# One decoder layer on one core: sample bias rows stored once a head and token, the sweep's weight loads issued by GpSimd, and a third eviction tile

## The chip, the cores and the metric

The kernel runs on one core of a Trainium2 chip. The metric is device time in microseconds of one execution. Three executions of the kernel before took 3164.48, 3169.32 and 3171.83 us; the median, 3169.32 us, is what the change is measured against.

## The reference

One inference step of one decoder layer, for a prompt of 2048 rows and for 8 x 4 = 32 sample rows that share all weights. In outline:

```
h = RMSNorm(x) @ w_in          # 1024 -> 9472 columns: q, k, v, za, u (GLU), zb, qc, zc, 3 merge gates
A: dilated window attention, 12 heads x 64, patterns (128,1), (512,4), (2048,16), combined by their denominators
B: GLU -> causal depthwise conv, width 31 -> LayerNorm -> swish
C: cross-attention, 4 heads x 128, into 256 memory rows
mix = sum over A, B, C of sigmoid(gate) * ((branch * silu(z)) @ w_proj)
y = x + RMSNorm(mix @ w_out)
```

In the sample path of A the 32 rows look into a cache of 1024 past keys. To each score comes a bias that depends on the head, on the token t = 0..3 (through the distance from the key), and on the pattern. All data is fp32. The outputs also hold the new key and value rows, the conv state and the memory keys and values.

## The kernel before, in words

**Products.** Every fp32 product is made of three matmuls on float32r parts: `gemm` (L156 to L164) multiplies the high part of the weights with the high and the low part of the activations, and the low part of the weights with the high part. `load_w` (L141 to L154) loads 128 columns of a weight (128 partitions x 8 blocks of 512 bytes, 512 KB) as `wraw` and splits it into `whi` and `wlo`; the split of the input projection's weights is done by GpSimd, in two instructions (L55, L56). Activations lie in SBUF by thirds of the rows (`THIRDS`: 768, 768, 544).

**Phases.** `phase_a1` (to about 860 us) normalises x, builds bias tables (`bias_rows`), and makes q, k, v, qc and the GLU with its convolution. Then three strands run side by side until about 2560 us: (1) `memory`, which holds `memory_kv`, the LayerNorm of the conv branch in chunks of 256 rows (`conv_norm`), the prompt's cross-attention and the sample's; then `sample_bias` and `sample_attention`; (2) `attention`, six pairs of heads; (3) `sweep`, which makes the remaining 40 blocks of 128 columns (za, zb, zc and the gates gt) for each third, and is the filler of the other two. `phase_c` then makes the output projections; it is not touched by the change.

**The order of the work.** The program is emitted strand after strand, and a planner with a simulated time line then orders each engine's instructions by priority; the sweep is emitted last and fills what the others leave. On the chip each engine, and each engine's queue of DMA issues, runs its list strictly in that order. A DMA that waits for a semaphore therefore holds back everything behind it on the engine that issues it.

**The sweep** (L1064 to L1080). Per third, X is reloaded by GpSimd (16 DMAs at L1072); per block, `load_w` is called with `q=nc.scalar`, so that ScalarE issues the load of `wraw` (L146). There are two `wraw`, two `whi` and two `wlo`: the load of block n+2 waits until GpSimd has read `wraw` of block n (the end of its L56). The chunks of a block (`SCHUNKS`: seven of 256 rows, one of 288) go through `chunk` (L223 to L242): 24 matmuls into one of two PSUM tiles `gg`, then ScalarE makes tanh into an eviction tile `st` (L237 for the gates, L239 for the z paths), for the z paths VectorE multiplies it with the PSUM tile (L240), and ScalarE issues the store of `st` (L242). In the sweep there are two `st` tiles of 128 x 384, of which a chunk uses 256 or 288 columns. An `st` is free when its store has landed, and a `gg` when L237 or L240 has read it.

**The sample bias.** `bias_rows` (L344) makes a table `exs` of 12 heads x 3 patterns x 752 values and stores it to DRAM in one DMA (L368). `sample_bias` (L678 to L700) builds for each pattern a tile `sb` of 112 partitions x 672: partitions 0 to 47 and 64 to 111 are (head, token), and a token's row is the table's row shifted by 3 - t. It does so with 56 loads that SyncE issues (L695, L696, L698), each for 12 partitions of one token; three copies on VectorE (L699) then spread four values per row from `sn`. The tiles are first read in `sample_attention` (L802, L803).

**The combine of a head pair** (`att_pair`, L407) uses two small tiles of 32 x 128: `mn` (L417) for the minimum over patterns and `wsum` (L425) for the sum of weights. `mn` is last read before `wsum` is first written, by the same engine.

Of the kernel before, what the change touches and what calls it, by code (L numbers as in the profile page):

```python
# [7 lines left out]
F32 = mybir.dt.float32  # L8
# [4 lines left out]
PSUM = bass.MemoryType.PSUM  # L13
# [6 lines left out]
HA, DA, EA = 12, 64, 768  # L20
# [3 lines left out]
NT_S = 752  # L24
# [4 lines left out]

GROUPS = [(0, 3), (3, 6), (6, 9), (9, 12), (12, 14), (14, 17)]  # L30
CHUNKS = [(0, 384), (384, 384), (768, 384), (1152, 384), (1536, 256), (1792, 288)]
SCHUNKS = [(256 * i, 256) for i in range(7)] + [(1792, 288)]
THIRDS = [(0, 768), (768, 768), (1536, 544)]

CQ, CK, CV, CZA, CUB, CZB, CQC, CZC, CGT = 0, 768, 1536, 2304, 3072, 4608, 5376, 5888, 6400
# [2 lines left out]
class K:  # L38
# [184 lines left out]
    def chunk(self, kind, j, s, n, w, stg, psg, tag, pst=None, q=None):  # L223

        nc = self.nc
        q = q or nc.sync
        p = psg.tile([128, 512], F32, name=tag)
        self.gemm(p[:, :n], w, [self.x_at(k, s, n) for k in range(8)])
        st = stg.tile([128, 384], F32, name="st")
        dst = dict(q=self.d_q, k=self.d_k, qc=self.d_qc, za=self.d_za, zb=self.d_zb, zc=self.d_zc, gt=self.d_g).get(kind)  # L230
        if kind in ("q", "k", "v", "qc"):
            sc = dict(q=-0.125, k=1.0, qc=float(np.float32(DC ** -0.5)), v=1.0)[kind]
            nc.scalar.activation(st[:, :n], p[:, :n], AF.Copy, scale=sc)  # L233
            if kind in "kv":
                self.rows_out(kind, j, s, n, st, stg, pst)
        elif kind == "gt":
            nc.scalar.activation(st[:, :n], p[:, :n], AF.Tanh, scale=0.5)  # L237
        else:
            nc.scalar.activation(st[:, :n], p[:, :n], AF.Tanh, scale=0.5)  # L239
            nc.vector.scalar_tensor_tensor(st[:, :n], st[:, :n], 1.0, p[:, :n], op0=ALU.add, op1=ALU.mult)  # L240
        if dst is not None:
            q.dma_start(dst[j][:, s:s + n], st[:, :n])  # L242
# [101 lines left out]
    def bias_rows(self, cpool, pool, psum):  # L344
        nc, I = self.nc, self.I
        rb = self.rb = cpool.tile([33, HA], F32, name="rb")
        nc.vector.memset(rb, 1.0e30)
        raw = pool.tile([32, HA], F32, name="rbr")
        nc.sync.dma_start(raw, I["rel_bias"])
        nc.vector.tensor_scalar(rb[0:32], raw, -1.0, None, op0=ALU.mult)  # L350
        oh = pool.tile([33, 3, 384], F32, name="oh")
        nc.sync.dma_start(oh, I["c_onehot"])
        ext = pool.tile([HA, 3, 384], F32, name="ext")
        for p in range(3):
            t = psum.tile([128, 512], F32, name="tr")
            nc.tensor.matmul(t[:HA, :384], rb, oh[:, p, :], start=True, stop=True)
            nc.vector.tensor_copy(ext[:, p, :], t[:HA, :384])
        nc.sync.dma_start(self.d_ext, ext)
        ohs = pool.tile([33, 3, NT_S], F32, name="ohs")
        nc.sync.dma_start(ohs, I["c_onehot_s"])  # L360
        exs = pool.tile([HA, 3, NT_S], F32, name="exs")
        for p in range(3):
            for c in range(0, NT_S, NT_S // 2):
                cs = slice(c, c + NT_S // 2)
                t = psum.tile([128, 512], F32, name="tr")
                nc.tensor.matmul(t[:HA, :NT_S // 2], rb, ohs[:, p, cs], start=True, stop=True)
                nc.vector.tensor_copy(exs[:, p, cs], t[:HA, :NT_S // 2])
        nc.sync.dma_start(self.d_exs, exs)  # L368
        pf = pool.tile([128, 3, 128], F32, name="permf")
        nc.sync.dma_start(pf, I["c_perm"])  # L370
        self.perm = cpool.tile([128, 3, 128], R32, name="perm")
        nc.vector.tensor_copy(self.perm, pf)
# [34 lines left out]
    def att_pair(self, hp):  # L407
        nc, ap, ps, ao = self.nc, self.ap, self.aps, self.ao
# [13 lines left out]
        nc.scalar.activation(e, e, AF.Exp, scale=-1.0)  # L422
        el = st[:, 3:6, :]
        nc.vector.tensor_mul(el, e, el)
        w = ao.tile([32, 128], F32, name="wsum")  # L425
        nc.vector.tensor_add(w, el[:, 0, :], el[:, 1, :])
        nc.vector.tensor_add(w, w, el[:, 2, :])
        nc.vector.reciprocal(w, w)
# [249 lines left out]
    def sample_bias(self, keep):  # L678

        nc = self.nc  # L680
        NK, R = 672, 112
        self.sbias = []
        for p in range(3):
            bt = keep.tile([R, NK], F32, name=f"sb{p}")
            nc.vector.memset(bt, 1.0e30 if p < 2 else 0.0)
            nw = keep.tile([R, 4], F32, name=f"sn{p}")
            nc.vector.memset(nw, 0.0)
            base = self.d_exs[:, p, :]
            for r in (0, 64):
                for t in range(4):  # L690
                    rows = slice(r + t, r + 48, 4)

                    def src(o, n):
                        return bass.AP(tensor=base.tensor, offset=base.offset + o, ap=[[base.ap[0][0], HA], [1, n]])
                    nc.sync.dma_start(bt[rows, 0:512], src(3 - t, 512))  # L695
                    nc.sync.dma_start(nw[rows, :], src(515 + 3 - t, 4))  # L696
                    if p == 2:
                        nc.sync.dma_start(bt[rows, 512:640], src(522 + 32 * (3 - t), 128))  # L698
            nc.vector.tensor_copy(bt[:, 640:NK].rearrange("p (b t) -> p b t", t=4), nw[:, None, :].to_broadcast([R, 8, 4]))  # L699
            self.sbias.append(bt)  # L700


    def sample_attention(self):
# [360 lines left out]
    def sweep(self, blocks, xp, wp, stg, ps):  # L1064
        nc = self.nc
        for th, (a, n) in enumerate(THIRDS):
            if th:
                X = ([], [])
                for k in range(8):
                    for c in range(2):  # L1070
                        t = xp.tile([128, 768], R32, name=f"x0{'hl'[c]}{k}")
                        nc.gpsimd.dma_start(t[:, :n], self.d_x[th][c][k])  # L1072
                        X[c].append(t)
                self.X[th] = X
            for kind, j in blocks:
                w = self.early.pop((kind, j), None) if th == 0 else None
                w = w or self.load_w(wp, self.win(self.BASE[kind] + 128 * j), 8, q=nc.scalar, bufs=2, rp=stg)
                for s, m in SCHUNKS:
                    if a <= s < a + n:
                        self.chunk(kind, j, s, m, w, stg, ps, "gg", q=nc.scalar)  # L1080
                        yield
# [108 lines left out]
    def build(self):  # L1190
        tc, nc = self.tc, self.nc
        with tc.tile_pool(name="dr", bufs=1, space=DRAM) as dp, tc.tile_pool(name="cst", bufs=1) as cp:
            self.scratch(dp)
            self.cpool = cp
            with tc.tile_pool(name="x0", bufs=1) as x0, tc.tile_pool(name="w1", bufs=2) as wp:
                self.X = [tuple([x0.tile([128, 768], R32, name=f"x0{c}{k}") for k in range(8)] for c in "hl"), None, None]
                self.phase_a1(wp)
                with tc.tile_pool(name="gst", bufs=2, reuse_waits="tile") as gp, tc.tile_pool(name="pgg", bufs=2, space=PSUM, reuse_waits="tile") as pgg:
                    blocks = [(k, j) for k, n in (("za", 6), ("zb", 6), ("zc", 4), ("gt", 24)) for j in range(n)]
                    self.filler, self.credit = self.sweep(blocks, x0, wp, gp, pgg), 0  # L1200
                    with tc.tile_pool(name="sbk", side="right", bufs=1, reuse_waits="tile") as sk:
# [7 lines left out]
    def scratch(self, dp):  # L1209
# [7 lines left out]
        self.d_c = t("d_c", [6, 128, T])  # L1217
        self.d_actb = t("d_actb", [6, 128, T])
        self.d_ext = t("d_ext", [HA, 3, 384])
        self.d_exs = t("d_exs", [HA, 3, NT_S])  # L1220
        self.d_st = [t(f"d_st{h}", [6, S]) for h in range(HA)]
        self.d_cf = [t(f"d_cf{j}", [3, 2 * S]) for j in range(6)]
        self.d_act = [None if 6 <= j < 12 else t(f"d_act{j}", [128, T]) for j in range(16)]
# [73 lines left out]
```

## Time and profile before

| | |
|---|---|
| median of three executions | 3169.32 us (3164.48 to 3171.83) |
| profiled execution | 3156.1 us; span 3154.0 us |
| TensorE busy | 2992.8 us, 95% of the span |
| VectorE, GpSimd, ScalarE busy | 65%, 43%, 36% |
| mean granted TensorE clock | 0.983 |

The profile is one execution. Times in it count from the start of its span. Busy shares leave out instructions that only issue a DMA or wait for a semaphore; a row whose engine is called ACTq or SPq is such an instruction in the queue of that engine. `[1.5 <-DVE st L240]` behind an instruction of the time line means that its engine sat idle for 1.5 us before it, until VectorE finished the instruction of line 240 that writes `st`. Such a releaser is inferred; where several were waited for, it is the last one.

### The profile page before, as it was taken

To read this page: it belongs to the slowest core of one execution; us is meant where nothing else is said; L and a number is where in the kernel's file an instruction comes from. 1 tells how busy PE (TensorE), PEld (TensorE's weight loads), DVE (VectorE), ACT (ScalarE), POOL (GpSimd) and SP (SyncE) were. 2 spreads that over 40 slices of the span, in tenths; PEclk is the share of its full clock that TensorE was granted. 3 is DMA by queue.
4 is the path that set the end of the run, shared out by engine and by line. 5 is a ranking of instruction groups with operands and counts; after the bars stand their busy time and mean duration, and the time that the engine had idled before them with its cause. 6 is when DMAs were issued, how large, how long until landed. Compare 5 with 4: busy or idle time off the path is not lost. (4 is left out here: it accounts for less than half of the span.)

```text
span 3154.0 us, 55551 instructions
## 1 busy us (share of the span) xinstructions
PE 2992.8 (95%) x20705; PEld 2837.2 (90%) x20705; DVE 2037.6 (65%) x3854; ACT 1123.6 (36%) x2835; POOL 1368.9 (43%) x1048
## 2 busy tenths in 40 slices
PE   7999999999977999999999999999999989999998
PEld 6899999999977899998999999999898967787897
DVE  5297797797677825565546667565757557555663
ACT  5110010010132423244447575665565532222221
POOL 0121322232455537444366666667776443233240
PEclk9999999999998999999999999999999999999999
DMA  6332222221255444468454556575655486657561
GB/s 224 111 100 83 80 60 61 63 63 64 90 162 166 127 140 144 147 213 251 144 142 118 151 139 159 123 196 144 166 140 149 117 283 210 226 172 220 158 206 53
DMA packets 532219, 454.67 MB, mean 144 GB/s; under 512 B 118191, under 2 KB 458581, under 8 KB 531137
## 3 DMA queue, kind: packets, MB, share of 16 engines
q1 hardware_dynamic: 357502, 335.36, 36.3%
q10 hardware_dynamic: 169840, 105.02, 11.6%
q0 software_dynamic: 4608, 10.75, 1.1%
q8 instruction: 164, 2.69, 0.4%
q14 instruction: 105, 0.86, 0.1%
HBM read 332.96 MB, written 118.04 MB: 143 GB/s over the span
## 5 line engine op out<-in xcount | busy, mean ns | idle before, releaser
L162 PE MATMUL gg<-x0h,whi 128*128 128x256 f32 (+1 forms) x2560 | 747.9, 292 | 33.9 <-DVE st L240 26.9
L164 PE MATMUL gg<-x0h,wlo 128*128 128x256 f32 (+1 forms) x2560 | 741.1, 290 | 5.7 <-POOL wlo L56 5.7
L163 PE MATMUL gg<-x0l,whi 128*128 128x256 f32 (+1 forms) x2560 | 742.3, 290 | 0.0
L55 POOL TENSOR_SCALAR whi<-wraw 128x1024 fp32r<-128x1024 f32 x162 | 221.4, 1368 | 918.0 <-PE g L163 534.7
L162 PEld LDWEIGHTS gg<-x0h,whi 128*128 128x128 f32 x2560 | 493.7, 193 | 42.2 <-DVE st L240 23.5
L164 PEld LDWEIGHTS gg<-x0h,wlo 128*128 128x128 f32 x2560 | 493.6, 193 | 8.3 <-POOL wlo L56 6.1
L163 PEld LDWEIGHTS gg<-x0l,whi 128*128 128x128 f32 x2560 | 493.9, 193 | 1.9 <-issue 0.3
L316 DVE SCALAR_TENSOR_TENSOR acc<-G,cw,acc 128x1536 f32<-128x1536 f32 (+15 forms) x354 | 461.8, 1336 | 0.0
L56 POOL TENSOR_TENSOR wlo<-wraw,whi 128x1024 fp32r<-128x1024 f32 x162 | 451.8, 2790 | 9.9 <-PE gg L164 0.5
L151 POOL TENSOR_TENSOR clo<-craw,chi 128x768 fp32r<-128x768 f32 (+1 forms) x96 | 172.6, 1799 | 352.9 <-ACT chi L150 338.1
L616 ACT ACTIVATE P<-T,stm 128x128 f32<-128x128 f32 (+1 forms) x576 | 260.7, 455 | 116.7 <-DVE stm L614 78.1
L233 ACT ACTIVATE st<-g 128x384 f32<-128x384 f32 (+1 forms) x132 | 60.3, 461 | 564.8 <-PE g L164 564.8
L614 DVE CUSTOM_DVE_ANT_0 T<-s,bias 128x128 f32<-128x128 f32 (+1 forms) x576 | 191.8, 357 | 78.3 <-PE s L606 44.6
L162 PE MATMUL pg<-ac,chi 128*128 128x512 f32 (+1 forms) x640 | 227.7, 358 | 14.9 <-ACT chi L150 7.9
L164 PE MATMUL pg<-ac,clo 128*128 128x512 f32 (+1 forms) x640 | 227.8, 358 | 6.2 <-POOL clo L151 6.2
L163 PE MATMUL pg<-ac,chi 128*128 128x512 f32 (+1 forms) x640 | 227.7, 356 | 0.7 <-DVE ac L1187 0.7
L164 PE MATMUL g<-x1h,wlo 128*128 128x384 f32 x544 | 186.2, 343 | 0.0
L163 PE MATMUL g<-x1l,whi 128*128 128x384 f32 x544 | 185.9, 342 | 0.0
L162 PE MATMUL g<-x1h,whi 128*128 128x384 f32 x544 | 183.0, 339 | 3.0 <-ACT x1h L131 3.0
L163 PE MATMUL g<-x0l,whi 128*128 128x384 f32 x544 | 184.9, 340 | 0.0
L164 PE MATMUL g<-x0h,wlo 128*128 128x384 f32 x544 | 183.7, 338 | 0.0
L162 PE MATMUL g<-x0h,whi 128*128 128x384 f32 x544 | 182.5, 337 | 0.0
(329 smaller groups left out, 7453.4 us busy)
## 6 DMA issues: line engine op xcount, KB each, us to landing
wraw<-in_w_in ACTq DMA_DIRECT2D x119, 512.0 KB
d_g<-st ACTq DMA_DIRECT2D x168, 128.0 KB
cb<-d_cf SPq DMA_DIRECT2D x72, 256.0 KB
g<-d_g SPq DMA_DIRECT2D x72, 256.0 KB
wraw<-in_w_in SPq DMA_DIRECT2D x35, 512.0 KB
kvc<-in_cache_k_win SPq DMA_DIRECT2D x8, 1536.0 KB
kvc<-in_cache_v_win SPq DMA_DIRECT2D x8, 1536.0 KB
raw<-d_q SPq DMA_DIRECT2D x48, 256.0 KB
```

Source lines behind the costliest of these rows:

```text
L55: nc.gpsimd.tensor_scalar(hi, raw, 1.0, 1.0, op0=ALU.mult, op1=ALU.mult)
L56: nc.gpsimd.tensor_sub(lo, raw, hi.bitcast(F32))
L151: nc.gpsimd.tensor_sub(lo, raw, hi.bitcast(F32))
L162: nc.tensor.matmul(ps, hi[:, k, :], h, start=k == 0, stop=False)
L163: nc.tensor.matmul(ps, hi[:, k, :], l, start=False, stop=False)
L164: nc.tensor.matmul(ps, lo[:, k, :], h, start=False, stop=k == kb - 1)
L233: nc.scalar.activation(st[:, :n], p[:, :n], AF.Copy, scale=sc)
L316: nc.vector.scalar_tensor_tensor(a3[:, lo:hi], G[:, src:src + hi - lo, 2 - m:130 - m], w, a3[:, lo:hi], op0=ALU.mult, op1=ALU.add)
L614: nc.vector.tensor_tensor_reduce(sc[:, :w], t[:, o:o + w], bias[:, 256 - w:256], 1.0, 3.0e38, ALU.add, ALU.min, m)
L616: nc.scalar.activation(P[:, o:o + w], sc[:, :w], AF.Exp, bias=m, scale=-1.0, accum_out=self.stl[:, col:col + 1])
```

## The change

There are five edits.

1. `bias_rows` writes the table in another form: `d_exs` is now 12 heads x 4 tokens x 3 patterns x 644, each token's row already shifted. Twelve stores take the place of one.
2. `sample_bias` keeps one tile `sb` of 112 x 3 x 672 and one `sn`; (head, token) is a single stride in DRAM, so that three loads for each half of the partitions, six in all, take the place of 56.
3. The sweep's `load_w` gets `q=nc.gpsimd`: GpSimd issues the 119 loads of `wraw` instead of ScalarE. The stores of `st` stay with ScalarE.
4. The pool `gst` has three buffers instead of two. `wraw` asks for two by itself and keeps them; `st` becomes three. The tile is 272 columns wide instead of 384 in the sweep, and the last two chunks become 272 + 272 rows instead of 256 + 288, so that the number of chunks, matmuls and columns stays.
5. `wsum` shares the buffer of `mn`.

```diff
-SCHUNKS = [(256 * i, 256) for i in range(7)] + [(1792, 288)]
+SCHUNKS = [(256 * i, 256) for i in range(6)] + [(1536, 272), (1808, 272)]
...
-        st = stg.tile([128, 384], F32, name="st")
+        st = stg.tile([128, 384 if tag == "g" else 272], F32, name="st")
...
-        nc.sync.dma_start(self.d_exs, exs)
+        for t in range(4):
+            nc.sync.dma_start(self.d_exs[:, t, :, 0:512], exs[:, :, 3 - t:515 - t])
+            nc.sync.dma_start(self.d_exs[:, t, :, 512:516], exs[:, :, 518 - t:522 - t])
+            nc.sync.dma_start(self.d_exs[:, t, 2, 516:644], exs[:, 2, 522 + 32 * (3 - t):650 + 32 * (3 - t)])
...
-        w = ao.tile([32, 128], F32, name="wsum")
+        w = ao.tile([32, 128], F32, name="mn")
...
+        bt = keep.tile([R, 3, NK], F32, name="sb")
+        nc.vector.memset(bt[:, 0:2], 1.0e30)
+        nc.vector.memset(bt[:, 2], 0.0)
+        nw = keep.tile([R, 3, 4], F32, name="sn")
+        nc.vector.memset(nw, 0.0)
+        src = self.d_exs.rearrange("h t p x -> (h t) p x")
+        for r in (0, 64):
+            nc.sync.dma_start(bt[r:r + 48, :, 0:512], src[:, :, 0:512])
+            nc.sync.dma_start(bt[r:r + 48, 2, 512:640], src[:, 2, 516:644])
+            nc.sync.dma_start(nw[r:r + 48], src[:, :, 512:516])
         for p in range(3):
-            bt = keep.tile([R, NK], F32, name=f"sb{p}")
...
-                    nc.sync.dma_start(bt[rows, 0:512], src(3 - t, 512))
-                    nc.sync.dma_start(nw[rows, :], src(515 + 3 - t, 4))
-                    if p == 2:
-                        nc.sync.dma_start(bt[rows, 512:640], src(522 + 32 * (3 - t), 128))
...
+            nc.vector.tensor_copy(bt[:, p, 640:NK].rearrange("p (b t) -> p b t", t=4),
+                                  nw[:, p, None, :].to_broadcast([R, 8, 4]))
...
-                w = w or self.load_w(wp, self.win(self.BASE[kind] + 128 * j), 8, q=nc.scalar, bufs=2, rp=stg)
+                w = w or self.load_w(wp, self.win(self.BASE[kind] + 128 * j), 8, q=nc.gpsimd, bufs=2, rp=stg)
...
-                with tc.tile_pool(name="gst", bufs=2, reuse_waits="tile") as gp, tc.tile_pool(name="pgg", bufs=2, space=PSUM, reuse_waits="tile") as pgg:
+                with tc.tile_pool(name="gst", bufs=3, reuse_waits="tile") as gp, tc.tile_pool(name="pgg", bufs=2, space=PSUM, reuse_waits="tile") as pgg:
...
-        self.d_exs = t("d_exs", [HA, 3, NT_S])
+        self.d_exs = t("d_exs", [HA, 4, 3, 644])
```

More of the change, by code (lines that the diff above doesn't have):

```diff
@@ L681, in sample_bias @@
         NK, R = 672, 112
-        self.sbias = []
-        for p in range(3):
-            bt = keep.tile([R, NK], F32, name=f"sb{p}")
[L685 to L696, printed above, removed]
-                    if p == 2:
-                        nc.sync.dma_start(bt[rows, 512:640], src(522 + 32 * (3 - t), 128))
-            nc.vector.tensor_copy(bt[:, 640:NK].rearrange("p (b t) -> p b t", t=4), nw[:, None, :].to_broadcast([R, 8, 4]))
-            self.sbias.append(bt)
+        bt = keep.tile([R, 3, NK], F32, name="sb")
[8 more added lines that the diff above has]
+            nc.sync.dma_start(nw[r:r + 48], src[:, :, 512:516])
+        for p in range(3):
+            nc.vector.tensor_copy(bt[:, p, 640:NK].rearrange("p (b t) -> p b t", t=4),
+                                  nw[:, p, None, :].to_broadcast([R, 8, 4]))
+        self.sbias = [bt[:, p] for p in range(3)]
     def sample_attention(self):
```

## The prediction

> **What bounds the kernel now.** I read the page first (how long is the span, which engine fills it), then busy time by stretch, then what TensorE waited for.
>
> ```profile
> span 3154.0 us, 55551 instructions
> PE 2992.8 (95%) x20705; PEld 2837.2 (90%) x20705; DVE 2037.6 (65%) x3854; ACT 1123.6 (36%) x2835; POOL 1368.9 (43%) x1048
> ```
> ```profile
> 860.00:1100.00 240.00, 195.62 (x1471) 188.01 (x1470) 191.24 (x239) 82.04 (x156) 133.32 (x121) 0.92 0.50 154
> 1100.00:1600.00 500.00, 481.00 (x3706) 455.30 (x3707) 256.41 (x525) 187.91 (x429) 224.65 (x262) 0.99 0.55 170
> 1600.00:2500.00 900.00, 863.83 (x7121) 854.47 (x7120) 577.54 (x1738) 558.52 (x1721) 592.98 (x477) 0.99 0.58 146
> 2500.00:2560.00 60.00, 53.05 (x402) 51.81 (x400) 24.79 (x24) 11.59 (x26) 33.08 (x18) 0.97 0.73 209
> ```
>
> The columns of the second fence are the stretch and its length, busy time and instructions of TensorE, its weight loads, VectorE, ScalarE and GpSimd, then the granted clock, DMA share and GB/s. TensorE is the bound: 95% of the span. The change touches what runs from 860 to 2560 us (and a few stores near 111 us). There the sweep is a filler that could use any gap, so a gap that is closed should come off the end, and a new one should go on it. The four rows give what can be won: 240 - 195.62 = 44.4 us idle, then 19.0, 36.2 and 7.0, together 106.6 us. The clock column adds something: at 0.92 the first stretch also runs its matmuls slower. The columns are the prediction's map: in the first stretch VectorE is busy 191 of 240 us, so TensorE waits on VectorE there; from 1600 on GpSimd is busy 593 of 900, which makes it the engine with the least room to take new work.
>
> ```profile
> PE gg L162 <- DVE st L240: 26.9, 17, 4.6
> PE s L605 <- POOL QS L480: 8.3, 6, 2.5
> PE gg L164 <- POOL wlo L56: 5.7, 2, 4.1
> PE pt L560 <- ACT P L616: 2.6, 4, 0.7
> PE gg L162 <- POOL whi L55: 1.1, 1, 1.1
> PE o L586 <- ACT ph L564: 0.6, 1, 0.6
> ```
>
> Each row is us in all, times, longest. The largest wait is for an eviction of the sweep; those on GpSimd come to 15.1 us in nine places, those on ScalarE in attention to 3.2 us.
>
> **The change part by part.** The sum is made against the profiled execution, 3156.1 us (span 3154.0 and 2.1 around it). It lies 13.2 us under the median of 3169.32; I carry the difference over to the median unchanged.
>
> *ScalarE no longer issues the weight loads.* An issue itself is 0.39 us, but what it holds back is the matter:
>
> ```profile
> L146 ACTq DMA_DIRECT2D wraw<-in_w_in x119: 380/390/1032, 871.6 to 2531.7; - x119
> L146 ACTq EVENT_SEMAPHORE  x97: 17/17/7369, 871.5 to 2530.9; - x97
> ```
> ```profile
> 871.61 1.87 ACTq L146 DMA_DIRECT2D wraw<-in_w_in  x2
> 873.53 1.06 ACT L904 ACTIVATE msq<-mt 128x1024 f32<-128x1024 f32 x1 [8.32 <-DMA sb<-d_exs]
> ```
> ```profile
> 876.08 2.83 DVE L662 TENSOR_REDUCE sm<-sq 128x256 f32<-128x1536 f32 x1 [5.90 <-ACT sq L660]
> ```
> ```profile
> 878.96 0.79 PE L664 MATMUL sco<-sm,ones 128*128 128x256 f32 x1 [5.59 <-DVE sm L662]
> ```
>
> The page puts the 8.32 us before L904 down to a DMA of `sb`, but what stands in ScalarE's queue right before is L146, whose longest semaphore wait is 7.37 us: the first loads wait for memory of the phase before. Behind them stand L904 and the square of the LayerNorm; then L662, then TensorE, idle for 5.59 us. VectorE was free for 5.90 us before L662, so with ScalarE free the whole chain moves forward, at most by TensorE's gap. I take 4 us, because L904 needs its own load and may still stand in front (bounds 0 and 5.6). GpSimd, which takes the wait over, has nothing else there.
>
> Elsewhere the loads' wait for GpSimd's L56 holds ScalarE; the tile view of `wraw` names who stood behind it:
>
> ```profile
>   ACT L63: 8.6, 2
>   ACT st L237: 7.4, 2
>   ACT ph L564: 4.8, 2
>   ACT P L616: 4.6, 2
>   ACT sP L993: 4.0, 1
> ```
>
> That is 29.4 us of ScalarE in nine waits. Most of it is not TensorE's: its own waits on ScalarE in attention are the 3.2 us above. I take 3 us (bounds 0 and 29.4). Only the wait goes; what is late next there is VectorE, which the same chains pass through.
>
> *A third eviction tile.* Two gaps end with an eviction that had waited for a store to land; in a third it is not clear:
>
> ```profile
> 1608.16 0.38 ACT L239 ACTIVATE st<-gg 128x256 f32<-128x256 f32 x1 [7.09 <-DMA d_zb<-st]
> ```
> ```profile
> 1609.05 0.38 PE L162 MATMUL gg<-x0h,whi 128*128 128x256 f32 x1 [1.72 <-DVE st L240]
> ```
> ```profile
> 2541.47 0.41 ACT L237 ACTIVATE st<-gg 128x288 f32<-128x288 f32 x1 [4.40 <-DMA d_g<-st]
> ```
> ```profile
> 2541.93 0.40 PE L162 MATMUL gg<-x0h,whi 128*128 128x288 f32 x1 [1.05 <-ACT st L237]
> ```
> ```profile
> 1125.63 0.36 PE L162 MATMUL gg<-x0h,whi 128*128 128x256 f32 x1 [3.10 <-DVE st L240]
> ```
>
> 1.72 + 1.05 go. Of the 3.10 at 1125 I take half, since ScalarE also has a LayerNorm square in front of those evictions. That is 4.3 us (bounds 2.8, and the 26.9 + 1.05 of all eviction waits). The other waits on L240 lie where VectorE is full, and a third `st` doesn't free a PSUM tile: there are still two. The 272-wide chunks change neither the number of matmuls nor of columns: 0.
>
> *The sample bias.*
>
> ```profile
> L695 SPq DMA_DIRECT2D sb<-d_exs x24: 690/700/3548, 863.7 to 920.2; - x24
> L696 SPq DMA_DIRECT2D sn<-d_exs x24: 691/700/1099, 865.6 to 921.0; - x24
> L699 DVE COPY sb<-sn x3: 501/1409/1919, 887.9 to 923.1; 112x32 f32<-112x32 f32 x3
> L368 SPq DMA_DIRECT2D d_exs<-exs x1: 323/323/323, 111.5 to 111.5; - x1
> ```
> ```profile
>   DMA sb<-d_exs: 3.1, 2
>   DMA sn<-d_exs: 1.1, 1
> ```
>
> With the eight like loads of L698 (for the last pattern alone), 56 issues at 0.70 us are 39 us of SyncE between 864 and 922; six are 4 us. SyncE isn't on TensorE's path, but VectorE waited 4.2 us for these loads in three places (the last two rows, of the tile view of `sb`), in the stretch where TensorE waits on VectorE. I take 2 us (bounds 0 and 4.2). On the other side eleven more stores of 0.32 to 0.70 us, 3.5 to 8 us of SyncE, stand at 111 us ahead of the loads of the first weights. TensorE is busy without a break soon after; I take 0, and 8 us if that cover isn't there. `wsum` in the buffer of `mn`: the same engine in order, 0.
>
> *GpSimd issues 119 loads.* The nearest row is its reload of X:
>
> ```profile
> L1072 POOL DMA_DIRECT2D x0l<-d_x x16: 527/536/746, 1452.1 to 2126.3; - x16
> L56 POOL TENSOR_TENSOR wlo<-wraw,whi x162: 2346/2400/9049, 19.9 to 2546.3; 128x1024 fp32r<-128x1024 f32 x162
> L56 POOL TENSOR_TENSOR wlo<-wraw,whi 128x1024 fp32r<-128x1024 f32 x162 | 451.8, 2790 | 9.9 <-PE gg L164 0.5
> q0 software_dynamic: 4608, 10.75, 1.1%
> ```
>
> An X load is 0.54 us and, by the queue's row, 4608 / 32 = 144 packets; a weight load has 128 x 8 rows of 512 bytes, some 1040. If only the issue counts, 0.54 us; if the time goes with the pieces, 0.54 x 1040 / 144 = 3.9 us. I take 1.0: 0.54 for the issue, and 0.39 by which the mean of L56 (2790 ns) is over its median (2400), as what GpSimd's instructions here lose to company. It is much nearer to the first end, because the row's own X loads of 384 and 272 KB don't differ. 119 x 1.0 is 119 us in 1700, of which GpSimd is now busy 984 (the four rows). TensorE sees it only where it waits on GpSimd: nine places, and a load in front in about half, so +4.5 us (bounds 2.4 at 0.54 in half, 35 at 3.9 in all nine). Queued behind a load on GpSimd are the Q and V splits of attention; it may itself be queued behind their waits, with a block's length of slack.
>
> [...] No run yet shows a load of that many pieces.
>
> The sum: -4 - 3 - 4.3 - 2 + 4.5 = -8.8 us. With a gap goes lost clock: in the first stretch 8% of 240 us, 19 us, go with 44.4 us idle, 0.43 us for each; the 4 and the 2 us lie there, so 2.6 more. In all -11.4: 3156.1 becomes 3144.7, and the median 3158 us.
>
> **The rivals.**
>
> *GpSimd comes late (slower).* The place is the head of each pair in attention, where QS, V, `whi` and `wlo` stand in one queue. VectorE and GpSimd hold each other up now:
>
> ```profile
> 931.46 12.61 DVE L674 SCALAR_TENSOR_TENSOR c<-sq,c 128x1536 f32<-128x1536 f32 x1 [2.14 <-ACT sq L673]
> 903.26 1.74 DVE L674 SCALAR_TENSOR_TENSOR c<-sq,c 128x1536 f32<-128x1536 f32 x1
> ```
>
> The same instruction took 1.74 and 12.61 us. If issues are held like this, at 3.9 us some 63 loads from 1600 to 2500 (119 by share of time) add 246 to the 593 busy us, 839 of 900: GpSimd is then as full as TensorE. The term becomes +35, the sum about +19 (the gains stay): 3188 us. It decides from about 1.8 us an issue, where the term in all nine places (16 us) eats the gains of 15.9. For it: the wide ends above. Against: X loads follow each other without a break. [...]
>
> *VectorE keeps the gaps (no change).* In the first stretch VectorE is 80% busy and TensorE's waits name it; a freed ScalarE then only waits for VectorE, and the 4, 3 and 2 us are not seen. 4.3 remains against 4.5 for GpSimd: 3169 us. That the third tile does nothing since two PSUM tiles hold is part of this case.
>
> *More of the eviction waits go.* If most of the 26.9 us on L240 come from ScalarE held by loads and stores, 20 of them go instead of 4.3, and with fewer gaps the clock of 0.92 rises to 0.96, 4% of 196 us or 8 more: 3158 - 16 - 8 = 3134 us. For it: ScalarE's 29.4 us. Against: VectorE's load.
>
> **How the numbers follow.** The measurement of this kernel can tell about 0.2%, 6.3 us, from no change. The forecast has 0.42 and its own range is 3148 to 3167; the larger gain 0.15, no change 0.22, GpSimd late 0.21. Since the planner orders all engines' lists anew, each case is uncertain by some 8 us (estimate: two of the longer gaps, 4.6 + 4.1, appear or vanish). The range, 3124 to 3188, reaches to the larger gain less this, and to the centre of the slower case, leaving out its upper half and a little below. Faster than 3163: most of the first two, 0.55; within 0.2%: 0.23; slower: 0.22.
>
> **What would show it.** Right: L146 on GpSimd at about 1.0 us; no ScalarE idle ended by `wlo` and none by a store of `st`; the gap before L664 near 879 us under 2 us; six loads of `sb` and `sn`; idle TensorE from 860 to 2560 about 95 us instead of 106.6; waits on QS, `whi` and `wlo` 20 instead of 15.1 us. Wrong: an issue of 2 us or more, GpSimd over 75% busy from 1600 on, and QS waits that double (then GpSimd late); or ScalarE free and the idle sum of the first stretch still 44 us (then VectorE kept it).

## The result, and the profile after

The change makes the kernel slower: a median of 3191.6 us in eleven runs (3177.6 to 3197.7) against 3169.3 in eleven of the kernel before (3160.1 to 3180.3), a ratio of 1.0074 (95% interval 1.0056 to 1.0093). The forecast was 3158 with a range of 3124 to 3188.

The page of the kernel after: the span, busy time by engine, and the queue of the DMAs that GpSimd issues (packets, MB, share).

```profile
span 3189.7 us, 55428 instructions
PE 3017.2 (95%) x20705; PEld 2859.7 (90%) x20705; DVE 2053.7 (64%) x3851; ACT 1125.4 (35%) x2835; POOL 1463.1 (46%) x1167
q0 software_dynamic: 21744, 73.15, 8.3%
```

TensorE has the same 20705 instructions and is 24.4 us longer busy with them. So the longer span is hardly idle time. The clock says where it comes from: the profiled execution before had a mean granted clock of 0.983, this one 0.972, and span times clock is 3100 us in both (3154.0 x 0.983, 3189.7 x 0.972). Below I call that product the *full-clock time*: roughly the span had the clock never been lowered. Over all runs it is 3106.3 us after and 3099.5 before (uncertain by about 3 and 2), at mean clocks of 0.9747 and 0.9789; the two figures of the kernel before are from the 29 runs of it beside experiments 5 to 8, since no clock is known for its eleven here. Some 7 us of the loss are therefore work and gaps, and 13 to 14 us are clock (3106.3/0.9747 - 3106.3/0.9789 = 13.7). One execution of the eleventh kernel below took 12753 us instead of some 3166 and is left out of its figures.

Busy time by stretch after, with the columns of the prediction's second fence (stretch, length, TensorE, its loads, VectorE, ScalarE, GpSimd, clock, DMA share, GB/s):

```profile
860.00:1100.00 240.00, 193.22 (x1422) 184.17 (x1421) 190.26 (x232) 79.09 (x152) 142.02 (x126) 0.89 0.50 148
1100.00:1600.00 500.00, 485.43 (x3746) 459.94 (x3746) 254.38 (x525) 191.15 (x433) 258.96 (x303) 0.99 0.55 170
1600.00:2500.00 900.00, 852.18 (x6860) 841.51 (x6858) 577.67 (x1674) 535.39 (x1647) 620.01 (x525) 0.96 0.57 143
2500.00:2560.00 60.00, 60.00 (x492) 59.99 (x491) 29.97 (x81) 30.38 (x87) 33.59 (x28) 1.00 0.46 129
```

Two rows got worse. In the first, the clock is 0.89 instead of 0.92 and 49 matmuls fewer were done. In the third, attention, idle time of TensorE is 47.8 us instead of 36.2, the clock 0.96 instead of 0.99, and 261 matmuls fewer were done. The sum of idle time looks the same as before (109.2 against 106.6) only because the sweep, being late, now fills the last row.

**What came as forecast.** The tile views of `wraw`, of `sb` and of `sn`, kernel after (min/median/max in ns; then who waited for the splits, us and times):

```profile
L146 POOL DMA_DIRECT2D wraw<-in_w_in x119: 884/930/1082, 841.9 to 2565.9; - x119
...
  POOL wraw L146: 18.7, 53
```
```profile
L697 DVE COPY sb<-sn x3: 173/175/175, 880.0 to 880.1; 112x32 f32<-112x32 f32 x3
L693 SPq DMA_DIRECT2D sb<-d_exs x2: 543/600/657, 863.7 to 872.5; - x2
L694 SPq DMA_DIRECT2D sb<-d_exs x2: 328/394/461, 867.0 to 873.8; - x2
```
```profile
L695 SPq DMA_DIRECT2D sn<-d_exs x2: 538/552/565, 868.5 to 874.2; - x2
```

An issue takes GpSimd 0.93 us, 1.0 was taken; never over 1.08. In addition 53 issues waited 0.35 us each for GpSimd's own split. The copies of the bias went from 1.41 to 0.175 us. From 860 to 2560 us no eviction on ScalarE waits for a split any more, and none for a store of the sweep (three do at the sweep's late end, 12.4 us in all). The gap of 5.59 us before L664 (L668 in the kernel after) is gone. This is the timeline of VectorE, then of TensorE, of the kernel after (start, length, instruction, idle time before it):

```profile
871.94 2.91 DVE L666 TENSOR_REDUCE sm<-sq 128x256 f32<-128x1536 f32 x1 [1.23 <-ACT sq L664]
```
```profile
874.90 0.70 PE L668 MATMUL sco<-sm,ones 128*128 128x256 f32 x2 [0.21 <-DVE sm L666]
```

**What took its place.** Four microseconds later stands a longer gap, which the timelines of TensorE and of GpSimd show:

```profile
887.53 0.58 PE L162 MATMUL gg<-x0h,whi 128*128 128x256 f32 x1 [8.69 <-DVE mrs L67]
```
```profile
841.90 1.98 POOL L146 DMA_DIRECT2D wraw<-in_w_in  x2
881.49 1.04 POOL L55 TENSOR_SCALAR whi<-wraw 128x1024 fp32r<-128x1024 f32 x1 [37.61 <-DVE st L240]
...
884.93 2.55 POOL L55 TENSOR_SCALAR whi<-wraw 128x1024 fp32r<-128x1024 f32 x2
```

VectorE's L67 is only what ended last by the profile; TensorE's matmul reads `whi`. The loads of the sweep left at 841.9, but GpSimd's list has splits of two blocks of `w_mem_kv` in front of theirs, and SyncE issues the first of those loads only at 874.8. So GpSimd stands idle for 37.6 us, though its loads of 841.9 and 843.0 had landed within 6.3 us, and splits the memory's blocks at 881.49 and 884.93. The sweep's split is the second of the last row's two and ends just before 887.5; until then the sweep, which should fill 878.8 to 887.5, has no `whi`. In the kernel before, whose load left only at 871.6, the sweep's block was the first in that list:

```profile
875.97 1.05 POOL L55 TENSOR_SCALAR whi<-wraw 128x1024 fp32r<-128x1024 f32 x1 [33.69 <-DMA wraw<-in_w_in]
```

This gap is not the price of GpSimd's issue, though. With ScalarE issuing and all else as in the change (the ninth kernel below), gaps of 5.53 and 9.23 us stand between 874 and 897, and the first stretch comes out no better:

```profile
860.00:1100.00 240.00, 194.12 (x1445) 186.42 (x1444) 193.54 (x243) 81.51 (x156) 133.91 (x118) 0.89 0.52 155
```

Its clock is 0.89 with the six bias loads alone too (the third), and 0.92, as before, with GpSimd's issue alone (the first). So the loss of the first row goes with the six loads emitted in this place, whoever issues the weights.

In attention, three of the eleven gaps over 2 us end with something of GpSimd's, and a drop of the clock follows each. TensorE's timeline of the kernel after around one of them:

```profile
1820.02 0.48 PE L609 MATMUL s<-KH,QS 128*128 128x128 f32 x1 [2.69 <-POOL QS L484]
...
1821.90 0.41 PE L163 MATMUL gg<-x0l,whi 128*128 128x256 f32 x1
...
1826.15 0.28 PE L162 MATMUL gg<-x0h,whi 128*128 128x256 f32 x1
```

and the stretches that hold the three, after (then before), with the clock behind GpSimd's column:

```profile
1820.00:1840.00 20.00, 19.98 (x145) 19.98 (x146) 9.84 (x38) 11.90 (x35) 17.96 (x15) 0.85 0.49 119
2140.00:2160.00 20.00, 19.30 (x123) 18.83 (x123) 12.48 (x48) 13.47 (x49) 12.15 (x16) 0.74 0.90 230
2340.00:2360.00 20.00, 16.72 (x117) 16.51 (x116) 7.92 (x29) 9.63 (x31) 13.37 (x14) 0.83 0.43 95
```
```profile
1820.00:1840.00 20.00, 20.00 (x177) 19.99 (x175) 13.15 (x42) 15.23 (x47) 12.39 (x10) 1.00 0.64 150
2140.00:2160.00 20.00, 19.21 (x157) 19.01 (x156) 10.06 (x34) 10.23 (x31) 11.57 (x13) 1.00 0.38 105
2340.00:2360.00 20.00, 20.00 (x165) 19.86 (x164) 10.49 (x16) 8.91 (x23) 15.39 (x15) 1.00 0.69 188
```

A gap of 2.69 us for `QS` is followed by 6 us in which the same matmul takes 0.41 instead of 0.28 us. The second is 2.4 us for the reload of X, which GpSimd issues in both kernels, the third 3.28 us again for `QS`. The gaps themselves are 8.3 us; the lowered clock adds 20 x (0.15 + 0.26 + 0.17) = 11.6 us.

Before both gaps for `QS`, GpSimd was not busy but idle:

```profile
1816.41 0.61 POOL L55 TENSOR_SCALAR V<-rv 128x512 fp32r<-128x512 f32 x1 [6.62 <-DMA d_act<-O]
```
```profile
2347.15 0.61 POOL L55 TENSOR_SCALAR V<-rv 128x512 fp32r<-128x512 f32 x1 [6.29 <-DMA d_g<-st]
```

A split of V stands in front of `QS` in its list. By the semaphores it waited for the last of the loads of `rv`, which SyncE had issued at 1811.11 and 2341.19 and which landed 4.9 and 5.6 us later. These two gaps come from a late load and the order of GpSimd's list, not from the time that its issues take.

### The profile page after: what moved, and what is told of

Its sections match the earlier page's. It is cut to its first block, busy times and chain, and to the rows that moved or that the text cites. A ratio compares the mean times of both kernels' runs of the same rounds, so it can differ in the third digit from the quotient of the medians.

```text
span 3189.7 us, 55428 instructions
## 1 busy us (share of the span) xinstructions
PE 3017.2 (95%) x20705; PEld 2859.7 (90%) x20705; DVE 2053.7 (64%) x3851; ACT 1125.4 (35%) x2835; POOL 1463.1 (46%) x1167
## 3 DMA queue, kind: packets, MB, share of 16 engines
q0 software_dynamic: 21744, 73.15, 8.3%
q8 instruction: 164, 2.69, 0.4%
## 4 chain that ended last, share of the span: by engine, by line
PE 71%; DMA 11%; DVE 7%; POOL 4%; issue 3%; ACT 2%; SPq 1%; ACTq 0%; POOLq 0%; DVEq 0%
PE g L162 8%; PE g L163 8%; PE g L164 8%; PE gg L162 6%; PE gg L163 6%; PE gg L164 6%; DMA cb<-d_cf 3%; PE pg L164 3%; PE pg L162 3%; PE pg L163 3%; PE pt L564 2%; PE y L1167 2%; PE y L1168 2%; PE y L1166 2%; PE o L591 1%
## 5 line engine op out<-in xcount | busy, mean ns | idle before, releaser
L162 PEld LDWEIGHTS gg<-x0h,whi 128*128 128x128 f32 x2560 | 497.4, 194 | 38.9 <-DVE st L240 13.7
L162 PE MATMUL pg<-ac,chi 128*128 128x512 f32 (+1 forms) x640 | 229.2, 359 | 16.9 <-ACT chi L150 11.6
L569 DVE TENSOR_TENSOR pl<-pt,ph 128x512 fp32r<-128x512 f32 x240 | 155.0, 651 | 50.7 <-ACT ph L568 48.9
```

Of the source, the lines that this page charges most:

```text
L162: nc.tensor.matmul(ps, hi[:, k, :], h, start=k == 0, stop=False)
L569: nc.vector.tensor_tensor(pl[:, :w], t[:, :w], ph[:, :w].bitcast(F32), op=ALU.subtract)
```

## The experiments

Two theories stood at the start. One: GpSimd's issue is what costs, whatever else is changed. The other: any edit makes the planner lay the lists anew, and the time is a throw of those lists. All runs are compared with the kernel before on the same chip; "full-clock" is the mean of span times clock against that of the kernel before beside it (uncertain by some 3 us; 8 and 5 in runs 17 and 18, of which there are five and six), "clock" the mean (before: 0.979).

| | kernel | ratio (95%) | full-clock, us | clock |
|---|---|---|---|---|
| | the change | 1.0074 (1.0056-1.0093) | +6.8 | 0.9747 |
| 1 | GpSimd's issue alone | 1.0039 (1.0021-1.0056) | +7.8 | 0.9772 |
| 2 | third tile alone | 0.9984 (0.9967-1.0000) | -5.5 | 0.9789 |
| 3 | six bias loads alone | 1.0040 (1.0025-1.0055) | -3.1 | 0.9741 |
| 4 | null: a planner constant | 1.0005 (0.9985-1.0026) | -0.2 | 0.9783 |
| 5 | null: patterns in reverse | 0.9989 (0.9974-1.0004) | -0.4 | 0.9801 |
| 6 | before, bias emitted first | 1.0060 (1.0041-1.0078) | -3.5 | 0.9722 |
| 7 | null: one more fill | 1.0003 (0.9989-1.0017) | +0.3 | 0.9791 |
| 8 | six loads, emitted first | 0.9968 (0.9954-0.9983) | -8.5 | 0.9788 |
| 9 | the change, ScalarE issues | 0.9978 (0.9964-0.9992) | -11.8 | 0.9769 |
| 10 | the change, bias first | 0.9995 (0.9976-1.0015) | -7.2 | 0.9770 |
| 11 | 9 with bias first | 0.9981 (0.9967-0.9995) | -7.0 | 0.9775 |
| 12 | 8 with GpSimd's issue | 1.0003 (0.9989-1.0017) | -4.3 | 0.9767 |
| 13 | before + fills on GpSimd | 0.9989 (0.9971-1.0007) | -2.5 | 0.9792 |
| 14 | 8 + fills on GpSimd | 0.9974 (0.9959-0.9989) | -12.3 | 0.9772 |
| 15 | before, SyncE issues | 1.0007 (0.9992-1.0021) | -5.4 | 0.9766 |
| 16 | 8, SyncE issues | 0.9969 (0.9953-0.9986) | -9.6 | 0.9790 |
| 17 | before + spare DMAs on GpSimd | 1.0123 (1.0102-1.0145) | +21.2 | 0.9734 |
| 18 | 8 + spare DMAs on GpSimd | 1.0106 (1.0086-1.0126) | +17.4 | 0.9742 |

**The parts alone (1 to 3).**

```
1:  -  ..., 8, q=nc.scalar, bufs=2, rp=stg)      +  ..., 8, q=nc.gpsimd, bufs=2, rp=stg)
2:  SCHUNKS, the width of st, wsum in mn, and bufs=3, as in the change; nothing else
3:  d_exs, its stores and sample_bias, as in the change; nothing else
```

> The kernel before with only the sweep's weight loads moved to GpSimd. Issue theory (GpSimd's 119 issues of 0.93 us, and the wait for its own L56 before them, make it late in attention): 3187 to 3195 us, all of the loss, TensorE's gaps from 1600 on as in the changed kernel. Order theory (the planner's new lists put the gaps where they cost clock, and any part redraws them): anywhere from 3160 to 3195 us, granted clock times span about 3100 as in both kernels. Prediction as it stood: about 3166 us.

> The kernel before with only the third eviction tile, its 272 columns, the two 272-row chunks and the shared small tile. Issue theory: no loss, 3160 to 3169 us. Order theory: differs from before by up to 25 us either way, with waits of ScalarE for stores of the eviction tile gone. Prediction as it stood: about 3165 us.

> The kernel before with only the new form of the sample's bias rows, six loads in place of 56. Issue theory: no loss, 3163 to 3169 us. Order theory: differs from before by up to 25 us either way; the first stretch from 860 to 1100 us shows another order of GpSimd's weight splits. Prediction as it stood: about 3167 us.

GpSimd's issue alone gives half of the loss. The tile view of `wraw`, then the attention stretch, with GpSimd's issue alone:

```profile
L146 POOL DMA_DIRECT2D wraw<-in_w_in x119: 892/930/1257, 843.0 to 2559.2; - x119
```
```profile
1600.00:2500.00 900.00, 852.24 (x6945) 840.58 (x6944) 593.62 (x1708) 544.66 (x1682) 633.36 (x534) 0.98 0.58 144
```

As in the kernel after, 47.8 us of idle time. The bias alone also costs, by as much, but in another way: its full-clock time is below the kernel before; what it loses is clock. The three parts sum to 0.63%, where the change has 0.74%. So the first theory, in its strict form, has failed: GpSimd's issue is not all of the loss, and a part without it costs as much.

**How much a new list is worth (4, 5, 7).** Edits that do nothing, and were meant to let the planner order anew.

```
4:  -  LAG = 900      +  LAG = 907          # a constant of the planner
5:  for p in (2, 1, 0)       # sample_bias, in place of range(3)
7:  +  nc.vector.memset(nw, 0.0)            # a second time, for each pattern
```

> The kernel before with the planner's lag for the convolution at 907 instead of 900 and no other change: the same instructions, perhaps in another order. Order theory: if the lists differ from before, the time moves by 0.2% or more. Issue theory: 3165 to 3173 us, as before.

> The kernel before with the three bias patterns built in the order 2, 1, 0: the same instructions, but new lists on all engines. Order theory: off the kernel before by 0.2% or more in one direction or the other, the difference lying after 1600 us too, where nothing of the bias is left, and span times granted clock still about 3100. Work theory (the loss of the bias form comes from its own loads): 3163 to 3170 us, as before.

> The kernel before with the memset of the small bias tile done twice (three instructions of 0.06 us on VectorE more): new lists. Order theory: off by 0.2% or more either way. Work theory: within 0.2%, 0.2 us of work.

The times moved by 0.05%, 0.11% and 0.03%, all within their intervals. But none of the three is a test of a new order: in the traces, the matmuls of TensorE, named by the tiles that they read and write, stand in another order than before at only 63, 456 and 0 of 20705 places, where GpSimd's issue alone (1) changes 9505. The test came with SyncE's issue (15 and 16, below): it changes the order of the kernel before at 10232 places and that of the eighth at 8725, and the time by 0.07% and 0.01%. So a new order is not in itself a dear throw, which is against the second theory in its strict form. That an edit's worth has nothing of such a throw in it is not shown: it changes with its company, as the third tile does, which is worth -0.16% alone, -0.62% beside six loads emitted second (9 against 3), and +0.13% and -0.08% beside six emitted first (11 against 8, 10 against 12).

**The place of the bias strand (6, 8).**

```
-  self.memory()                     +  self.sample_bias(sk)
-  self.sample_bias(sk)              +  self.memory()
```

> The kernel before with its 56 bias loads emitted ahead of the memory strand instead of behind it: the same instructions, new lists. Order theory: off the kernel before by 0.2% or more either way. Work theory: within 0.2%, since the loads are needed only at about 1320 us.

> The six bias loads alone, as in the experiment with the bias form alone, but emitted ahead of the memory strand. Order theory: the 0.4% of that experiment is not a property of the loads, so this one comes out elsewhere, by 0.2% or more, and may be no slower than before. Work theory: 0.4% slower again, 3177 to 3183 us.

With 56 loads emitted first, the loads of the memory rows stand behind them on SyncE. The first stretch, then the longest wait of TensorE in it, of the kernel before with the bias emitted first:

```profile
860.00:1100.00 240.00, 166.38 (x1225) 160.54 (x1224) 168.04 (x204) 72.66 (x130) 116.70 (x106) 0.83 0.45 138
```
```profile
PE tr L913 <- DVE mt L909: 41.3, 1, 41.3
```

With six loads there is nothing to stand behind. The same stretch with the six loads alone, emitted second as in the change, and, in the next fence, emitted first:

```profile
860.00:1100.00 240.00, 194.39 (x1444) 186.66 (x1444) 194.56 (x243) 81.61 (x156) 133.41 (x117) 0.89 0.53 155
```
```profile
860.00:1100.00 240.00, 197.60 (x1529) 190.65 (x1528) 197.61 (x253) 86.05 (x163) 137.21 (x122) 0.94 0.55 163
```

Clock 0.94 and 0.89, and 85 matmuls between them: the form of the six loads gains 0.32% in one place and loses 0.40% in the other, and the two differ in how the gaps of this stretch lie. The 85 matmuls are some 11 us (at 194.39/1444 us each), half of the difference of 23. In the change the place makes about the same difference (1.0074 and, in the tenth, 0.9995); with the third tile and ScalarE issuing it makes none (ninth and eleventh).

**Who issues the loads (9 to 12, 15, 16).** One word differs within each pair.

```
9:   the change with q=nc.scalar      10: the change, bias first      11: 10 with q=nc.scalar
12:  8 with q=nc.gpsimd               15: before with q=nc.sync       16: 8 with q=nc.sync
```

> The changed kernel with the weight loads given back to ScalarE (bias form and third tile stay). Issue theory: 0.4% faster than the changed kernel, about 3179 us. Order theory: with the bias form's lists, which alone came to 3180 us, and new ones for the tile, anywhere from 3160 to 3190 us.

> The changed kernel, all five edits, with the sample's bias emitted ahead of the memory strand. Order theory: well under the changed kernel's 3191 us, 3160 to 3180 us, though every instruction of the change is in it. Issue theory: 0.4% above the next run, which has the loads on ScalarE.

> The run before with the weight loads on ScalarE: bias form first, third tile. Order theory: 3150 to 3180 us and not always below its twin with GpSimd. Issue theory: 0.4% below its twin. It may be the fastest version, near 3155 us.

> Six bias loads emitted first (3159 us with the loads on ScalarE and two tiles), plus the weight loads on GpSimd. Issue theory: 0.4% slower, about 3172 us. Order theory: either sign, by up to 0.6%.

> The kernel before with the sweep's weight loads issued by SyncE in place of ScalarE: ScalarE is freed of its issues as in the change, and GpSimd has none. Theory that GpSimd's issue is what costs, and the freed ScalarE gains little: 0.997 to 1.000. If taking the loads off ScalarE's list is itself the cost (the load no longer stands behind the stores that free the tiles, and loads and stores share less of an order): 1.003 to 1.005. Lists: 0.994 to 1.006.

> SyncE's issue on the kernel with six bias loads emitted first (0.9968). GpSimd's issue the cost: 0.994 to 0.998, at or below that kernel. Taking the loads off ScalarE the cost: 1.000, as with GpSimd (1.0003). Lists: 0.991 to 1.003.

In four pairs GpSimd is slower than ScalarE, by 0.39, 0.96, 0.35 and 0.14 points (the last within its uncertainty of 0.24). Against SyncE it is slower by 0.32 and 0.34 (uncertain by some 0.23 each). SyncE against ScalarE is 0.07 and 0.01: within the intervals it makes no difference (0.9969 is where it was expected if GpSimd's issue is the cost, 1.0007 just above). So taking the loads off ScalarE is free of cost, and gives no time either; giving them to GpSimd costs, by how much depends on the rest of the kernel. The attention stretch shows where. With SyncE, on the kernel before and on the eighth:

```profile
1600.00:2500.00 900.00, 866.44 (x7133) 857.26 (x7133) 591.73 (x1749) 558.65 (x1723) 594.03 (x473) 0.98 0.56 144
```
```profile
1600.00:2500.00 900.00, 872.67 (x7158) 864.03 (x7158) 579.13 (x1745) 561.40 (x1725) 589.47 (x476) 0.98 0.58 146
```

and with GpSimd on the eighth, then with ScalarE in the change:

```profile
1600.00:2500.00 900.00, 852.19 (x6905) 841.62 (x6904) 574.98 (x1689) 540.86 (x1664) 628.76 (x533) 0.97 0.57 144
```
```profile
1600.00:2500.00 900.00, 863.09 (x7018) 852.36 (x7017) 568.11 (x1708) 546.26 (x1680) 583.01 (x475) 0.98 0.58 146
```

Idle time (900 less the first number) is 33.6 and 27.3 us with SyncE, 36.9 with ScalarE in the change and 36.2 in the kernel before, and 47.8 us with GpSimd in three kernels. ScalarE on the eighth has 43.5. In the tenth, whose pair differs least, it is 41.5, against 42.5 of its pair. So in the three pairs that differ clearly, and against SyncE, the idle time of this stretch goes the way of the cost; in the fourth it doesn't. By itself it is no proof: each number is from one execution, and the third tile alone has 47.0 us, and makes it good elsewhere.

**What of GpSimd's issue costs (13, 14, 17, 18).** These were to tell GpSimd's own time from the place of the load in its list.

```
13, 14:  + for _ in range(7):
         +     nc.gpsimd.memset(self.dm, 0.0)          # 128 x 32, per weight block
         (13 also has wsum in the buffer of mn, as the change does)
17, 18:  + nc.gpsimd.dma_start(self.d_dd.pop()[:, 0:16], self.win(c0)[:, 0:16])
```

> The kernel before, ScalarE issuing the loads as it did; GpSimd does seven small fills of a spare tile ahead of each weight block, some 0.9 us a block, the time that its issue of a load took. Theory that GpSimd's own time is the cost: 1.003 to 1.004 of the kernel before, as with GpSimd's issues alone (1.0039), and idle time of GpSimd's splits as there. Theory that it is the place of the load in GpSimd's list, behind splits that wait for tiles (the load goes out later): no cost, 0.998 to 1.002. Theory that the lists, planned anew, make it: anything from 0.994 to 1.006, without a common sign with the same fills in the six-load kernel.

> The same seven fills a block on the kernel with six bias loads emitted first (0.9968 of the kernel before). GpSimd's own time: 1.000, 0.35 per cent above that kernel, as GpSimd's issues there (1.0003). Place of the load in the list: 0.995 to 0.999. Lists: anywhere between 0.991 and 1.003.

> The kernel before with one more DMA a weight block (119 in all), issued by GpSimd: 1024 pieces of 64 bytes from the weight to scratch memory that nothing reads and that waits for nothing; ScalarE still issues the loads of the weights. It leaves no part of the computation out. Theory that making the pieces on GpSimd is the cost (it holds GpSimd, or VectorE beside it, longer than fills of the same length did): 1.003 to 1.005 of the kernel before, and a longest subtraction of KL above 4 us, as where GpSimd issued the loads (4.6 to 6.8 us against 2.2 to 3.5 elsewhere). Theory that it is the load's place in GpSimd's list, between its splits, with the wait for the split just before it: 0.998 to 1.001. Lists planned anew: 0.994 to 1.006.

> The same spare DMAs on the kernel with six bias loads emitted first (0.9968). Making the pieces the cost: 1.000, as with GpSimd's loads there (1.0003). Place in the list: 0.995 to 0.999.

All four missed the stretch that they were to probe. The tile views of the fills (thirteenth) and of the spare DMAs (seventeenth):

```profile
L1079 POOL MEMSET dm<- x840: 117/125/689, 0.7 to 198.1; 128x32 f32 x168
```
```profile
L1079 POOL DMA_DIRECT2D d_dd<-in_w_in x119: 755/755/1230, 1.3 to 173.1; - x119
```

Nothing waits for them and they wait for nothing, so the planner moved every one to the first 200 us, ahead of the sweep. They say nothing on GpSimd's time from 860 us on, and the expectation of the last two, which took the first two for an answer, had no ground. What they do show is that 840 fills there cost nothing while 119 spare DMAs of 0.755 us cost 1.2 to 1.4%, more than any theory had allowed. That loss lies ahead of the sweep: of the first 200 us TensorE is busy for 143 in the seventeenth and for 174 in the kernel before, and the sweep's first load leaves at 923.1 instead of 871.6. It says nothing on attention.

## Why the prediction was wrong

**ScalarE freed: 4 + 3 us, worth nothing.** The steps came: the gap before L664 closed and no eviction waits for a split any more. But a closed gap did not come off the end. It closed in the change, in the first and in the fifteenth kernel, and in each another one stood before TensorE within 15 us: 8.69, 5.19 and 9.10 us. Where the six loads come first, that place has a gap of 6.4 to 8.0 us whoever issues the weights. The same edit with SyncE, which costs GpSimd nothing, moves the time by 0.07% and 0.01%. In full-clock time it gains 5.4 and 1.2 us, and on the kernel before the lowered clock (0.9766) takes it back.

**GpSimd's issues: the term that was mis-sized.** Its price of an issue was right (0.93 for 1.0), in part by luck: it was made of 0.54 us and 0.39 us of being held up, but the quickest of the 119 issues took 0.884, so almost all of it is the same in every issue. And "TensorE sees it only where it waits on GpSimd: nine places" was wrong. Waits of TensorE that the profile names after GpSimd's `QS`, `whi` and `wlo` fell from 15.1 to 6.5 us from 860 to 2560, where 20 were forecast, while its idle time in attention rose by 11.6. The new idle time stands under other names, VectorE's above all. TensorE's waits from 1600 to 2500 in the kernel after (the first row came to 3.7 us before):

```profile
PE o L591 <- DVE pl L569: 14.9, 8, 4.0
PE s L609 <- DVE stm L618: 7.9, 7, 2.8
PE s L609 <- POOL QS L484: 6.0, 2, 3.3
```

Against SyncE the issue measures 13.2 and 5.4 us of full-clock time (each uncertain by some 4), not 4.5; against ScalarE, with that engine's gain in it, 7.8, 18.6, 4.2 and -0.2, in the mean +7.6, where gains of 7 and a cost of 4.5 made -2.5.

**"With a gap goes lost clock": the step that failed with the wrong sign.** I let the clock gain 2.6 us; it lost 13 to 14. I took the sum of idle time as the measure, at 0.43 us of clock for each. In the first stretch that sum rose by only 2.4 us (to 46.8), yet the clock fell from 0.92 to 0.89, some 7 us of 240. The gaps lie otherwise there: the 5.59 us went, one of 8.69 came, and TensorE was busy 4.67 us of the 20 from 880 on at a clock of 0.50. In attention, behind the gap of 2.69 us, the granted clock was 0.50 from 1820 to 1826, where the same matmul takes 0.41 instead of 0.28 us, and 0.99 from 1826 to 1832. Behind one of 3.01 us in the kernel before it did not fall (see below): here the length of a gap alone does not tell whether the clock falls.

**The third tile: right alone, not everywhere.** -4.3 was forecast, from evictions that wait for a store. With the tile alone those waits of ScalarE fell from 38.8 to 3.7 us from 860 to 2560, and TensorE's for L240 from 26.9 to 14.5. In full-clock time it measures -5.5 alone, -8.6 beside the six loads (the ninth against the third, -11.8 and -3.1), and +1.4 and -3.0 where the bias is first, which is nothing within the uncertainty. In time alone it is 0.9984, at the edge of its interval.

**The sample bias: right in work, wrong in time.** -2 was forecast; it is -3.1 us of full-clock time alone and -8.5 emitted first. But alone, in the place that it has in the change, it costs 0.40% (13 us), all of it clock. That its loads would shift the gaps of the first stretch, for 0.3 to 0.4% either way, was in no term. The "8 us" that I allowed for new lists was more than SyncE's new order moved (0.07%, 2 us) and less than the place of one strand did (0.72%, 23 us).

**The rivals.** The time came out near "GpSimd comes late" (3188), but not by its mechanism: the longest issue took 1.08 us in the change and 1.26 in the first kernel, GpSimd is 69% busy from 1600 on, not over 75, and the `QS` waits fell. The range's lower end was 2 us off by its own rule: 3134 less 8 is 3126.

**What stays open.** That giving the loads to GpSimd costs is shown by pairs that all have one sign, one of them within its uncertainty, and not by lists held equal. Which part of it costs is not shown: its 0.93 + 0.35 us between splits that TensorE soon needs, the place of the load in GpSimd's list, or VectorE held up beside a busier GpSimd. The two gaps for `QS` speak for an order, there that of the splits, but they are 6.0 us. Also, 0.96 of the fourfold comparison is well over the other three. The first stretch does not explain it, being as bad in the ninth kernel; attention, with 47.8 us idle at a clock of 0.96 against 36.9 at 0.98, holds it at least in part. A load held in place by a dependence, as a fill that reads the `wraw` just split, was not tried.

The fastest kernel found is the eighth, six bias loads emitted before the memory strand with ScalarE issuing, at 0.9968 (0.9954 to 0.9983); SyncE's issue adds nothing to it (0.9969).

## What to carry to other kernels

Multiply the span by the mean granted clock before explaining a difference: if the products agree, look for where gaps lie otherwise, not for added work. Before moving an issue to another engine, ask what that engine runs between the waits of others, and try the move on two engines: the one that is idle tells what the freed engine is worth, the difference tells what the new one pays. An operation put in as a probe must hang on something, or a planner moves it out of the stretch it should probe. And before a null edit is taken for a measure of reordering, count in the trace how much it reordered.

## What was not expected of the hardware

Three gaps of 2.4 to 3.3 us on TensorE were followed by 5 to 10 us of matmuls at 0.41 instead of 0.28 us, so that they cost over twice their length (8.3 us, and 11.6 by the clock). Not every such gap does: this one, in attention in the kernel before, was followed by matmuls at full speed (granted clock 1.00 from 2395 to 2405).

```profile
2398.25 0.33 PE L605 MATMUL s<-KH,QS 128*128 128x128 f32 x1 [3.01 <-DVE stm L614]
2398.41 0.28 PE L606 MATMUL s<-KL,QS 128*128 128x128 f32 x1
```

One VectorE subtraction (L469) looks as if it were held by several GpSimd instructions in a row. In the kernel after, two of them from 2045.57 on took 5.71 us, one of these 4577 ns where the median is 1628, beside a run of GpSimd without a break until 2049.06; it ended 1.1 us after that, about the 1.2 us of the quickest. The row of the tile `KL`, VectorE's timeline, then GpSimd's:

```profile
L469 DVE TENSOR_TENSOR KL<-raw,KH x24: 1211/1628/4577, 1634.7 to 2466.9; 128x1024 fp32r<-128x1024 f32 x24
```
```profile
2045.57 5.71 DVE L469 TENSOR_TENSOR KL<-raw,KH 128x1024 fp32r<-128x1024 f32 x2 [0.41 <-ACT KH L468]
```
```profile
2044.72 0.94 POOL L146 DMA_DIRECT2D wraw<-in_w_in  x1
2045.69 2.37 POOL L484 TENSOR_SCALAR QS<-QS 128x512 fp32r<-128x512 f32 x4
2048.03 1.03 POOL L55 TENSOR_SCALAR whi<-wraw 128x1024 fp32r<-128x1024 f32 x1
```

The longest such subtraction was 4.6 to 6.8 us in the four kernels in which GpSimd issues the loads (the change, 1, 10, 12) and 2.2 to 3.5 in the other sixteen. That is a sign of the third of the open parts, and no more: with SyncE's issue the long two-input operations of VectorE in attention (`KL`, and the three lines on `O` of 128 x 1024) took 107.6 us in all, as in the kernel after (107.3), at no cost in time.

The same load cost GpSimd 0.93 us to issue, ScalarE 0.39 and SyncE 0.38 (medians of L146 in the kernel after, in the one before and in the fifteenth), and the queues cut it differently. ScalarE's queue before, then after:

```profile
q10 hardware_dynamic: 169840, 105.02, 11.6%
```
```profile
q10 hardware_dynamic: 46080, 42.62, 4.3%
```

It lost 123760 packets over 119 loads, 1040 each, as I had counted them; GpSimd's queue gained 17136 (21744 - 4608), 144 each, as many as for a reload of X (4608 / 32). So the upper end of my price, 3.9 us from 1040 pieces, had nothing under it.
